# A hybrid encoder layer on one core: the three products of each split fp32 matmul in another order, and the zero matmuls of the v projection left out

## The chip, the cores and the metric

The kernel runs on one core of a Trainium2 chip. A core has a matrix engine (PE, with the loading of its weights shown apart as PEld), a vector engine (DVE), a scalar engine (ACT), a general engine (POOL) and a queue engine (SP) that issues the transfers between HBM and the on-chip memory. The metric is the device time of one execution in microseconds.

## What is computed

One encoder layer over two sequences, 1024 tokens (prompt) and 256 tokens (sample), width 2048, in fp32:

```python
def hybrid_layer(x, norm_w, w_in, na_rpb, conv_w, conv_b, gate_b, head_norm_w, w_out):
    hn = rmsnorm(x, norm_w)
    proj = jnp.einsum('btd,dp->btp', hn, w_in)
    na_q, na_k, na_v, na_g, ml_qk, ml_v, ml_o, ml_z, ml_gp = jnp.split(proj, cuts, axis=-1)
    att = neighbourhood_attention(na_q..., na_k..., na_v..., na_rpb)
    att = (att * jax.nn.silu(na_g)).astype(x.dtype)
    qk = jax.nn.silu(centred_depthwise_conv(ml_qk, conv_w, conv_b))
    ...
    h = bidirectional_mlstm(mq, mk, mv, gates)
    h = rmsnorm(h, head_norm_w...)
    mem = (h * jax.nn.sigmoid(ml_o) * jax.nn.silu(ml_z)).astype(x.dtype)
    mixed = jnp.concatenate([att, mem], axis=-1)
    return x + jnp.einsum('btm,md->btd', mixed, w_out)
```

The trunk ends with another RMSNorm. The two large products are `hn @ w_in` (2048 by 9232) and `mixed @ w_out` (2048 by 2048).

## The kernel before

Every fp32 product is made of three matmuls. An operand is split into a high half h, the value rounded to the matmul's reduced fp32 format (a cast on ACT), and a low half l, the rest (a subtraction on DVE); the product is h times h, plus h times l, plus l times h. The product of the two low halves is left out. In a matmul the stationary operand (128 by 128) is loaded into the engine, the moving operand (128 by up to 512 columns) is streamed through it, and the result is added up in one of eight banks of 512 fp32 columns per partition. Each matmul here comes with its own load of the stationary operand, also where that operand is the same as in the matmul before.

The tokens are taken in two groups: A, the first 768, and B, the last 512. The kernel has these stages, one after another on PE:

- Stage one projects group A (line 188, streams of 384 columns). The change doesn't touch it.
- The mixed stage, from about 1112 us, projects group B: the v columns by `proj_v` (names `wsv`, `pv`, line 583) and the others by `proj_pair` (names `ws`, `pc`, line 499). It does so beside attention and mLSTM of both sequences.
- The late gates are calls of `proj_pair` for gate columns that are applied at once.
- The output projection (`out_mm`, names `m_`, `ws_o`, `po`, line 1215) runs over three groups of 4, 4 and 2 token tiles of 128.

`proj_pair` makes two output tiles of 128 columns by 512 tokens, j = 0 and 1, each in a bank of its own, out of a ring of three banks (tag "pr"). The depth of 2048 is taken in four pieces r. For each piece SP loads 512 KB of weights into one of two buffers (`wr`), and `w_split` makes of each half of it, one for each j, a tile `ws` with high and low half: `t[:, 0]` starts the tile, `t[:, 1]` lies 544 columns on. The ring of these tiles has four places, shared with the tiles of `proj_v`. Here the weights are the stationary operand and the x tile, 512 tokens, the moving one. For each j the 12 matmuls of a piece run over four slices of depth with three products each, in the order (w0, xh), (w0, xl), (w1, xh), before the other j begins. When the pair ends, DVE takes both banks out with the scale of the tokens (line 165).

`out_mm` has the parts the other way round: the mixed activations `m` (128 tokens) are stationary and the output weights (512 columns) move, in the order (mh, w0), (mh, w1), (ml, w0). For each of four blocks of 512 columns and each slice of depth it runs over the token tiles of the group; the last four slices of depth (eight in the last block of the last group) are held back, and are run tile by tile, so that the tiles end one after another.

`proj_v` has x stationary and the weights moving with 256 columns. Two token tiles share a bank, so before the first product of a bank a matmul with a tile of zeros (`zer`, line 581) is written over all its 512 columns, with the start mark; the products then all add to it. For the head group that also makes the gates, each token tile has its own bank and there is no zero matmul.

The order in which the instructions stand on each engine isn't the written one: a scheduler places them by its own estimate of the times, within the dependencies. Within an engine they then run strictly in that order, and each waits for the counters that it was given.

Of the kernel before, what the change touches and what calls it, by code (L numbers as in the profile page):

```python
# [9 lines left out]
F32R = mybir.dt.float32r  # L10
# [3 lines left out]
P = 128  # L14
# [24 lines left out]
def kernel(  # L39
# [23 lines left out]
    def f(ap):  # L63
        return ap.bitcast(F32)
# [379 lines left out]
    for i, n1 in enumerate(order):  # L444
# [3 lines left out]
        k = i - 4  # L448
# [11 lines left out]
        tri(late.tile([P, P], F32, tag=n, name=n), cm, 0, (0.0, NEG))  # L460
        for n, cm in (("mask_f", -1), ("mask_b", 1))
    )
    zer = late.tile([P, P], F32R, tag="zer", name="zer")
    G.memset(f(zer), 0.0)

    xp1 = ctx.enter_context(tc.tile_pool(name="xp1", bufs=1))

# [11 lines left out]
    def w_split(raw, lo_, hi_, name, keep=False):  # L479
# [5 lines left out]
        split(t[:, 0, :n], t[:, 1, :n], raw[:, lo_:hi_])  # L485
        return t

    def proj_pair(n1, X, late=False):
        pb = [bank("pr", f"pc{n1}_{j}") for j in range(2)]
        for r in range(4):  # L490
            raw = w_piece(w_in[n1 // 2, r], f"{n1}_{r}")
            for j in range(2):
                t = w_split(raw, j * 512, j * 512 + 512, f"{n1}_{r}{j}")
                for f_ in range(2):
                    for q in range(2):
                        xh, xl = X.get(8 * f_ + 2 * r + q)
                        c = (2 * f_ + q) * P
                        for wi, xs in ((0, xh), (0, xl), (1, xh)):
                            PE.matmul(  # L499
                                pb[j], t[:, wi, c : c + P], xs,  # L500
                                start=r == 0 and f_ == 0 and q == 0 and wi == 0 and xs is xh,
                                stop=r == 3 and f_ == 1 and q == 1 and wi == 1,
                            )
        out = []
        for j in range(2):
            o = po(f"pco{n1}_{j}")
            if QK0 <= n1 < OT0:
                ct = n1 - QK0 + j
                DM.dma_start(o[:, 0:4], qb[ct])
                for z in (260, 518):  # L510
                    G.memset(o[:, z : z + 2], 0.0)
                out_scaled(
                    o[:, 4:].rearrange("p (s c) -> p s c", s=2)[:, :, :256],
                    pb[j].rearrange("p (s c) -> p s c", s=2),
                    rbs[1].rearrange("p (s c) -> p s c", s=2), n1,
                )
                cv = po(f"pcv{n1}_{j}")
                for _ in conv_taps(cv, o, ct, 516, 0):
                    pass
                DM.dma_start(cD[ct][:, GA - 2 : TP], cv[:, 0:258])  # L520
                DM.dma_start(cD[ct][:, TP:], cv[:, 260:516])
                continue
            o = o[:, :GB]
            out_scaled(o, pb[j], rbs[1], n1)
            if not late:
                DM.dma_start(pT[n1 + j][:, GA:], o)
            out.append(o)
        return out
# [21 lines left out]
    def proj_v(u, X):  # L550
        gates = u == NA_H // 2
        w = 272 if gates else 256
        nt = GB // P
        if gates:
            outs = [bank("a", f"pv{u}_{i}")[:, :w] for i in range(nt)]
        else:
            pb = [bank("pr", f"pv{u}_{i}") for i in range(nt // 2)]
            outs = [pb[t // 2][:, (t % 2) * 256 : (t % 2) * 256 + 256] for t in range(nt)]
        for r in range(4):
            raw = w_piece(w_in[NCH // 2 + u, r], f"v{u}_{r}")  # L560
            rawv = raw.rearrange("p (j f q c) -> p f q j c", j=2, f=2, q=2)
            if gates:
                graw = wb.tile([P, 2, 2, 16], F32, tag="wgr", name=f"wg{r}", bufs=2)
                DM.dma_start(
                    graw, w_g.rearrange("p (f r q c) -> p f r q c", f=2, r=4, q=2)[:, :, r]
                )
            for f_ in range(2):
                t = wb.tile([P, 2, 544], F32R, tag="wsp", name=f"wsv_{u}_{r}_{f_}", bufs=4)
                t4 = t[:, :, : 2 * w].rearrange("p h (k c) -> p h k c", k=2)
                h2, l2 = (  # L570
                    t4[:, z, :, 0:256].rearrange("p q (j c) -> p q j c", j=2) for z in range(2)
                )
                split(h2, l2, rawv[:, f_])
                if gates:
                    split(t4[:, 0, :, 256:272], t4[:, 1, :, 256:272], graw[:, f_])
                for tt in range(nt):
                    for q in range(2):
                        first, last = r + f_ + q == 0, r == 3 and f_ == 1 and q == 1
                        xh, xl = X.get(8 * f_ + 2 * r + q)
                        if first and not gates and tt % 2 == 0:  # L580
                            PE.matmul(pb[tt // 2], zer, t[:, 0, :512], start=True, stop=False)
                        for m, (xs, wi) in enumerate(((xh, 0), (xh, 1), (xl, 0))):
                            PE.matmul(  # L583
                                outs[tt],
                                xs[:, tt * P : (tt + 1) * P],
                                t[:, wi, q * w : (q + 1) * w],
                                start=first and m == 0 and gates,
                                stop=last and m == 2 and (gates or tt % 2 == 1),
                            )
        rc = rcs[1]  # L590
        for tt in range(nt):
            o = wb.tile([P, 256], F32, tag="vo", name=f"vo{u}_{tt}", bufs=2)
            S.mul(o, outs[tt][:, :256], rc[:, tt : tt + 1])
            r0 = GA + tt * P
            DM.dma_start(vD[u][r0 : r0 + P, :], o)
            if gates:
                V.scalar_tensor_tensor(
                    gt[:, GA // P + tt, :], outs[tt][:, 256:272], rc[:, tt : tt + 1], gb_sb,
                    op0=ALU.mult, op1=ALU.add,
                )  # L600
# [550 lines left out]
    X = LazyX()  # L1151
# [52 lines left out]
    for g, (t0, n) in enumerate(OG):  # L1204
        mh, ml_ = [None] * KT, [None] * KT
        for k in range(KT):
            raw = ahead[k] if g == 0 and k in ahead else mix_raw(g, k)
            mh[k], ml_[k] = x_pair(k, f"m{g}_{k}")
            split(mh[k][:, : n * P], ml_[k][:, : n * P], raw)
        yt = [yp.tile([P, D], F32, tag="y", name=f"y{g}_{t}", bufs=5) for t in range(n)]  # L1210
        ss = [yp.tile([P, 4], F32, tag="ss", name=f"ss{g}_{t}", bufs=8) for t in range(n)]

        def out_mm(o, tt, k, t, first, last):
            for i, (xs, wi) in enumerate(((mh[k], 0), (mh[k], 1), (ml_[k], 0))):
                PE.matmul(  # L1215
                    o, xs[:, tt * P : (tt + 1) * P], t[:, wi, :512],
                    start=first and i == 0, stop=last and i == 2,
                )

        for nb in range(4):  # L1220
            held = []
            n_hold = 8 if (g, nb) == (2, 3) else 4
            banks = [bank("pr" if nb % 2 and i < 3 else "a", f"po{g}_{nb}_{i}") for i in range(n)]
            for kp in range(0, KT, 2):
                nm = f"o{g}_{nb}_{kp}"
                raw = yp.tile([P, 1024], F32, tag="wr", name=f"wr_{nm}", bufs=4)
                DM.dma_start(raw, w_o[nb, :, kp * 512 : kp * 512 + 1024])
                for q in range(2):
                    k = kp + q
                    t = w_split(raw, q * 512, q * 512 + 512, f"{nm}_{q}", KT - n_hold <= kp < KT - 4)  # L1230
                    if kp >= KT - n_hold:
                        held.append((k, t))
                        continue
                    for tt in range(n):
                        out_mm(banks[tt], tt, k, t, k == 0, False)
            for tt in range(n):
                for i, (k, t) in enumerate(held):
                    out_mm(banks[tt], tt, k, t, False, i == n_hold - 1)
                cs = slice(nb * 512, nb * 512 + 512)
                xr = yp.tile([P, 512], F32, tag="xr", name=f"xr{g}_{nb}_{tt}", bufs=4)  # L1240
                DM.dma_start(xr, xtok[(t0 + tt) * P : (t0 + tt + 1) * P, cs])
                V.tensor_tensor(yt[tt][:, cs], banks[tt], xr, op=ALU.add)  # L1242
                S.activation(xr, yt[tt][:, cs], AF.Square, accum_out=ss[tt][:, nb : nb + 1])  # L1243
                G.tensor_tensor(yt[tt][:, cs], yt[tt][:, cs], fnb[:, cs], op=ALU.mult)  # L1244
                if nb == 3:
                    finish(t0 + tt, yt[tt], ss[tt])
# [87 lines left out]
```

## Time and profile before

| | |
|---|---|
| median of 3 runs | 2664.28 us (2663.93 to 2666.6) |
| profiled execution | 2667.78 us |
| its span, from the first instruction to the last | 2666.1 us |
| matmuls of `pc` | 2688 |
| matmuls of `po` | 1920 |
| matmuls of `pv` with 256 or 272 columns, and with zeros | 1536 and 14 |
| HBM read and written | 322.28 MB and 66.13 MB |

In the rows of the profile, L12 is line 12 of the kernel; names stand as output, arrow, inputs, with the buffer numbers left out, so that `pc<-x_4h,ws` are all matmuls with the high half of x slice 4 and some weight tile. `po<-ws_o,m_5l` has the low half of m slice 5. Duration of a matmul is modelled: they are pipelined, and one begins before the last one's duration ends, so that the spacing of the starts is what sets the pace. Rows of stretches give their length, then for PE, PEld, DVE, ACT and POOL busy time and number of instructions, then the granted clock, the share of the transfer engines and GB/s. Rows of the chain give start and length in us, the work and its count. Rows of one line or one tile give minimum, median and maximum duration in ns, and first and last start. Rows that begin with a cause give the idle time in us that the cause ended, and the number of cases.

### The profile page before, as it was taken

The numbers are of one execution on the slowest core, as the hardware profiler recorded it, in microseconds if no ns is written. First come the engines' busy times: TensorE is split into PE (matmuls) and PEld (weight loads), VectorE is DVE, ScalarE is ACT, GpSimd is POOL, SyncE is SP. The second block draws the span as 40 slices with busy tenths as digits, with TensorE's granted clock in tenths as the row PEclk, the third lists the DMA queues.
The fourth block names the chain that finished last, engine by engine and source line by source line (L and its number), as shares of the span: only waits on it lengthen the run. The fifth ranks groups of instructions, "written<-read, shape, count | busy, mean of one in ns | idle before, by whom it ended". The sixth has DMA issues, their size and how long they took to land. (4 is left out here: it accounts for less than half of the span.)

```text
span 2666.1 us, 42804 instructions
## 1 busy us (share of the span) xinstructions
PE 2627.4 (99%) x14724; PEld 2410.9 (90%) x14724; DVE 1804.6 (68%) x3645; ACT 1307.2 (49%) x2995; POOL 617.9 (23%) x898
## 2 busy tenths in 40 slices
PE   8999999999999999999999999999999999999998
PEld 8999999999999999988998998998888888888876
DVE  7867878788877878773686686686567445353455
ACT  7534444444444444543765665666556223242344
POOL 0434444444444444200010010110010000020121
PEclk9999999999999999999999999999999999999999
DMA  6423333323323233534555655655644545354465
GB/s 210 153 71 127 105 118 105 113 90 100 100 84 108 95 96 99 173 113 158 180 177 174 198 174 165 207 160 176 201 161 154 189 143 197 111 187 165 135 229 168
DMA packets 206435, 391.24 MB, mean 147 GB/s; under 512 B 25952, under 2 KB 117256, under 8 KB 206088
## 3 DMA queue, kind: packets, MB, share of 16 engines
q1 hardware_dynamic: 206216, 388.49, 45.4%
q8 instruction: 116, 1.90, 0.3%
q14 instruction: 103, 0.84, 0.1%
HBM read 322.28 MB, written 66.13 MB: 146 GB/s over the span
## 5 line engine op out<-in xcount | busy, mean ns | idle before, releaser
L152 DVE TENSOR_TENSOR ws_o<-wr_o,ws_o 128x512 fp32r<-128x512 f32 x192 | 150.5, 798 | 145.7 <-ACT ws_o L151 144.0
L152 DVE TENSOR_TENSOR ws<-wr,ws 128x512 fp32r<-128x512 f32 x224 | 154.7, 693 | 130.7 <-ACT ws L151 128.9
L151 ACT CAST ws<-wr 128x512 fp32r<-128x512 f32 x224 | 138.2, 619 | 187.7 <-PE pc L499 151.4
L151 ACT CAST ws_o<-wr_o 128x512 fp32r<-128x512 f32 x192 | 116.1, 617 | 165.9 <-PE po L1215 140.5
L1244 POOL TENSOR_TENSOR y<-y,fnb 128x512 f32<-128x512 f32 x40 | 58.5, 1479 | 536.2 <-ACT xr L1243 536.0
L1242 DVE TENSOR_TENSOR y<-po,xr 128x512 f32<-128x512 f32 x40 | 26.6, 685 | 50.7 <-PE po L1215 50.6
L152 DVE TENSOR_TENSOR wsv<-wr_v,wsv 128x512 fp32r<-128x512 f32 x64 | 45.3, 710 | 22.5 <-ACT wsv L151 22.0
L1243 ACT ACTIVATE xr<-y 128x512 f32<-128x512 f32 x40 | 25.1, 627 | 69.3 <-DVE y L1242 69.3
L102 POOL TENSOR_SCALAR mls_0r<-mls_0r 128x2 f32<-128x2 f32 x4 | 0.9, 234 | 249.4 <-ACT mls_0jk L1092 249.4
L151 ACT CAST wsv<-wr_v 128x512 fp32r<-128x512 f32 x64 | 39.2, 616 | 38.2 <-PE pc L499 25.1
L165 DVE TENSOR_TENSOR pco<-pc,rstdb 128x512 f32<-128x512 f32 x48 | 32.9, 686 | 29.2 <-PE pc L499 29.2
L274 DVE SCALAR_TENSOR_TENSOR pcv<-pco,cw_sb,pcv 128x516 f32<-128x516 f32 x64 | 47.8, 755 | 0.5 <-ACT pcv L268 0.5
L499 PE MATMUL pc<-x_8h,ws 128*128 128x512 f32 x112 | 44.5, 397 | 0.0
L499 PE MATMUL pc<-x_15h,ws 128*128 128x512 f32 x112 | 44.5, 397 | 0.0
L499 PE MATMUL pc<-x_10h,ws 128*128 128x512 f32 x112 | 44.5, 397 | 0.0
L499 PE MATMUL pc<-x_3h,ws 128*128 128x512 f32 x112 | 44.5, 397 | 0.0
L499 PE MATMUL pc<-x_0h,ws 128*128 128x512 f32 x112 | 44.4, 397 | 0.0
L499 PE MATMUL pc<-x_13h,ws 128*128 128x512 f32 x112 | 44.4, 396 | 0.0
L499 PE MATMUL pc<-x_4h,ws 128*128 128x512 f32 x112 | 44.4, 396 | 0.0
L499 PE MATMUL pc<-x_6h,ws 128*128 128x512 f32 x112 | 44.4, 396 | 0.0
L499 PE MATMUL pc<-x_9h,ws 128*128 128x512 f32 x112 | 44.4, 396 | 0.0
L499 PE MATMUL pc<-x_7h,ws 128*128 128x512 f32 x112 | 44.4, 396 | 0.0
(1737 smaller groups left out, 8901.4 us busy)
## 6 DMA issues: line engine op xcount, KB each, us to landing
wr<-in_w_in_dram SPq DMA_DIRECT2D x112, 512.0 KB
wr_o<-in_w_o_dram SPq DMA_DIRECT2D x96, 512.0 KB
wr_v<-in_w_in_dram SPq DMA_DIRECT2D x32, 512.0 KB
xq<-in_xtok_dram SPq DMA_DIRECT2D x20, 512.0 KB
xr<-in_xtok_dram SPq DMA_DIRECT2D x40, 256.0 KB
out_dram<-y SPq DMA_DIRECT2D x18, 512.0 KB
mraw<-mx SPq DMA_DIRECT2D x32, 256.0 KB
xr<-in_xT_dram SPq DMA_DIRECT2D x16, 384.0 KB
```

The costliest lines, as they stand in the source:

```text
L102: G.tensor_scalar(out, ssum, 1.0 / count, EPS, op0=ALU.mult, op1=ALU.add)
L151: S.copy(hi, src)
L152: V.tensor_tensor(lo, src, f(hi), op=ALU.subtract)
L165: V.tensor_tensor(o, src, rb, op=ALU.mult)
L274: V.scalar_tensor_tensor(dst[:, a:n], src[:, a + j - pad : n + j - pad], cw_sb[:, ct, j : j + 1], dst[:, a:n], op0=ALU.mult, op1=ALU.add,)
L499: PE.matmul(pb[j], t[:, wi, c : c + P], xs, start=r == 0 and f_ == 0 and q == 0 and wi == 0 and xs is xh, stop=r == 3 and f_ == 1 and q == ...
L1242: V.tensor_tensor(yt[tt][:, cs], banks[tt], xr, op=ALU.add)
L1243: S.activation(xr, yt[tt][:, cs], AF.Square, accum_out=ss[tt][:, nb : nb + 1])
L1244: G.tensor_tensor(yt[tt][:, cs], yt[tt][:, cs], fnb[:, cs], op=ALU.mult)
```

## The change

In `proj_pair` both tiles of a piece are split first. Then, for each slice of depth, three products of j = 0 and three of j = 1 follow each other, those of j = 1 in the opposite order: (w0, xl), (w0, xh), (w1, xh), then with the other tile (w1, xh), (w0, xh), (w0, xl). In `out_mm` the order is (ml, w0), (mh, w0), (mh, w1) for even token tiles and the reverse for odd ones. In `proj_v` the zero matmul goes; the first product of the even token tile in a bank carries the start mark, and the odd one adds to the same bank without one. The tile of zeros and its memset go.

```diff
-    zer = late.tile([P, P], F32R, tag="zer", name="zer")
-    G.memset(f(zer), 0.0)
...
+    FORTH = ((0, 1), (0, 0), (1, 0))
+
     def proj_pair(n1, X, late=False):
         pb = [bank("pr", f"pc{n1}_{j}") for j in range(2)]
         for r in range(4):
             raw = w_piece(w_in[n1 // 2, r], f"{n1}_{r}")
-            for j in range(2):
-                t = w_split(raw, j * 512, j * 512 + 512, f"{n1}_{r}{j}")
-                for f_ in range(2):
-                    for q in range(2):
-                        xh, xl = X.get(8 * f_ + 2 * r + q)
-                        c = (2 * f_ + q) * P
-                        for wi, xs in ((0, xh), (0, xl), (1, xh)):
+            t = [w_split(raw, j * 512, j * 512 + 512, f"{n1}_{r}{j}") for j in range(2)]
+            for f_ in range(2):
+                for q in range(2):
+                    xs = X.get(8 * f_ + 2 * r + q)
+                    c = (2 * f_ + q) * P
+                    first, last = r + f_ + q == 0, r == 3 and f_ == 1 and q == 1
+                    for j, passes in enumerate((FORTH, FORTH[::-1])):
+                        for m, (wi, xi) in enumerate(passes):
                             PE.matmul(
-                                pb[j], t[:, wi, c : c + P], xs,
-                                start=r == 0 and f_ == 0 and q == 0 and wi == 0 and xs is xh,
-                                stop=r == 3 and f_ == 1 and q == 1 and wi == 1,
+                                pb[j], t[j][:, wi, c : c + P], xs[xi],
+                                start=first and m == 0, stop=last and m == 2,
                             )
...
-                        if first and not gates and tt % 2 == 0:
-                            PE.matmul(pb[tt // 2], zer, t[:, 0, :512], start=True, stop=False)
                         for m, (xs, wi) in enumerate(((xh, 0), (xh, 1), (xl, 0))):
...
-                                start=first and m == 0 and gates,
+                                start=first and m == 0 and (gates or tt % 2 == 0),
...
         def out_mm(o, tt, k, t, first, last):
-            for i, (xs, wi) in enumerate(((mh[k], 0), (mh[k], 1), (ml_[k], 0))):
+            for i, (wi, xi) in enumerate(((1, 0), (0, 0), (0, 1))[:: 1 if tt % 2 else -1]):
                 PE.matmul(
-                    o, xs[:, tt * P : (tt + 1) * P], t[:, wi, :512],
+                    o, (mh[k], ml_[k])[xi][:, tt * P : (tt + 1) * P], t[:, wi, :512],
                     start=first and i == 0, stop=last and i == 2,
                 )
```

## The prediction

> **What bounds the kernel now.** I read the page first, then the kernel in five stretches, then the chain of work that ended last, and then single groups of matmuls.
>
> ```profile
> span 2666.1 us, 42804 instructions
> PE 2627.4 (99%) x14724; PEld 2410.9 (90%) x14724; DVE 1804.6 (68%) x3645; ACT 1307.2 (49%) x2995; POOL 617.9 (23%) x898
> PEclk9999999999999999999999999999999999999999
> ```
>
> PE is busy 99% of the span and its clock is granted in full. The next view cuts the span into stage one (projection of the first 768 tokens), the mixed stage (second projection beside attention and mLSTM), the late gates, two groups of the output projection, and the last group.
>
> ```profile
> 0.00:1112.30 1112.30, 1093.23 (x6271) 1083.56 (x6272) 870.59 (x1562) 528.01 (x1239) 467.66 (x560) 1.00 0.35 113
> 1112.30:2066.00 953.70, 947.28 (x5897) 849.88 (x5897) 656.84 (x1689) 567.59 (x1360) 81.67 (x278) 1.00 0.55 172
> 2066.00:2207.00 141.00, 141.00 (x625) 115.83 (x624) 60.31 (x93) 39.57 (x68) 0.00 (x0) 1.00 0.45 157
> 2207.00:2535.00 328.00, 327.93 (x1432) 268.03 (x1431) 144.83 (x196) 112.20 (x217) 44.74 (x36) 1.00 0.51 163
> 2535.00:2666.00 131.00, 117.98 (x504) 93.58 (x503) 72.03 (x107) 59.84 (x113) 23.82 (x24) 0.97 0.59 198
> ```
>
> After the length stands PE's busy time. PE idles 6.4 us of the 953.7 in the mixed stage, nothing in the late gates, 0.1 in the first output groups, 13 in the last. So from 1112 us on the time is the number of matmuls times their spacing, and waits are worth little. The chain says the same, and from it the mean spacing can be had (start, length, instruction, count):
>
> ```profile
> 1994.62 5.46 DMA wr<-in_w_in_dram
> 2079.18 131.12 PE pc L499 x567
> 2210.30 173.77 PE po L1215 x759
> 2387.15 174.62 PE po L1215 x761
> ```
>
> The gate projection (pc) runs 567 matmuls at 131.12/567 = 231.3 ns, the output projection (po) 759 at 229.0 ns. Both stream 512 columns, in threes, so the difference must come from the order of the operands. The durations in undisturbed stretches show where (min/median/max):
>
> ```profile
> L499 PE MATMUL pc<-x_11h,ws x17: 389/397/397, 2110.1 to 2198.8; 128*128 128x512 f32 x17
> L499 PE MATMUL pc<-x_4h,ws x16: 389/393/397, 2110.3 to 2180.1; 128*128 128x512 f32 x16
> L499 PE MATMUL pc<-x_11l,ws x9: 396/396/396, 2109.8 to 2198.6; 128*128 128x512 f32 x9
> L1215 PE MATMUL po<-ws_o,m_5h x64: 389/392/395, 2223.9 to 2534.4; 128*128 128x512 f32 x64
> L1215 PE MATMUL po<-ws_o,m_5l x32: 388/388/388, 2224.3 to 2534.6; 128*128 128x512 f32 x32
> L188 PE MATMUL A58b<-xg,A58s x144: 334/334/335, 307.8 to 335.7; 128*128 128x384 f32 x144
> ```
>
> A modelled duration is the spacing to the next start plus a constant: in pc the three are 389, 396 and 397, mean 394, less 231.3 gives 162.7; in po 389, 395, 388, mean 390.7, less 229.0 gives 161.7. So there are two classes of step, some 227 ns and some 234, and I call the second dear. Write w0 and w1 for the high and low half of a weight tile (w0 starts the tile, w1 lies 544 columns on) and h, l for the halves of x. In pc the order is (w0,h) 389, (w0,l) 396, (w1,h) 397: the step into w1 and the step out of w1 are dear. In po it is (h,w0) 389, (h,w1) 395, (l,w0) 388: only the step out of w1 is dear. The last row but one says more: all 32 l matmuls took 388, those too that end a weight tile, after which both operands change. So a change of both operands alone isn't what costs. Stage one, with the same three products at 384 columns and its halves otherwise placed, has one class, 334.
>
> **The change part by part.** First, the zero matmuls:
>
> ```profile
> L581 PE MATMUL pv<-wsv,zer x14: 389/394/397, 1190.9 to 1773.9; 128*128 128x512 f32 x14
> ```
>
> 14 of them at 394 - 162 = 232 ns: 3.2 us off PE, in the mixed stage, where nothing else is the bound. The tile's memset on POOL goes too; POOL is busy 23% of the span and waits there, so I count nothing (uncovered, it would be a part of a microsecond, once). The v projection keeps its order otherwise.
>
> Second, the pair projection. The 2688 matmuls, 224 casts, 224 subtracts and 112 loads of weights stay. What moves is the order, which a scheduler makes; in the built program I counted steps between neighbouring pc matmuls. Steps between w0 and w1 fall from 836 in and 833 out to 515 and 524, since two w1 now stand side by side. That is 630 dear steps fewer at 396.5 - 389 = 7.5 ns: 4.7 us. Steps where both operands change fall from 1671 to 554. Bounds of this term: nothing (if each use of a w1 or l tile costs its 7.5 ns wherever it stands), and 1117 x 7.5 = 8.4 us (if every change of both costs). I take the middle, which is what the rows of both projections obey together; it is a rule read off, and its mechanism I don't know.
>
> Third, the output projection: 1920 matmuls, steps out of w1 fall from 630 to 354: 276 at 395 - 388.5 = 6.5 ns, 1.8 us. Bounds: nothing; and 630 - 44 = 586 steps that leave w1 with both operands changed, 3.8 us.
>
> What the new orders ask of others. A block of 24 matmuls now needs both tiles of a piece and frees both at its end, where before each was freed after its 12. Rows for the preparation:
>
> ```profile
> L151 ACT CAST ws<-wr x224: 602/621/660, 1132.9 to 2199.2; 128x512 fp32r<-128x512 f32 x112
> L152 DVE TENSOR_TENSOR ws<-wr,ws x224: 652/691/965, 1133.6 to 2199.9; 128x512 fp32r<-128x512 f32 x112
>   PE pc L499: 152.5, 96
>   DMA wr<-in_w_in_dram: 27.9, 12
> ```
>
> The last two rows tell what the idle engine waited for ahead of these: 152.5 us in 96 cases for PE to give a tile back, 27.9 us in 12 for the load. So preparation is mostly early. A block lasts 24 x 0.231 = 5.5 us; two casts and the last subtract take 2 x 0.62 + 0.69 = 1.9 us. With four tiles in the ring, the pair freed at the end of one block is refilled during the next, with 3.6 us to spare: nothing on the path. Without that cover the loss would be up to 1.9 us for each of 112 pieces.
>
> A pair also starts its second bank sooner after the last pair ended, and that bank waits for DVE to empty it:
>
> ```profile
> L165 DVE TENSOR_TENSOR pco<-pc,rstdb x48: 670/690/693, 1161.7 to 2210.3; 128x512 f32<-128x512 f32 x48
> ```
>
> In the written order this would be six matmuls, 1.4 us, against 0.69 us plus whatever DVE has in hand. In the built order of the late gates 14 matmuls of the first bank go ahead, 3.2 us, so again nothing; if one in four of the 28 pairs lost 0.7 us, 5 us.
>
> In the output projection the first matmul of an even tile now needs the low half of x, which DVE makes, and the low half of the weights only third instead of second. The waits that PE had:
>
> ```profile
> PE po L1215 <- DVE ws_o L152: 3.1, 5, 1.0
> PE mlp_1in L924 <- ACT mlp_1Cb L151: 1.7, 2, 1.1
> ```
>
> Five waits for that low half become up to two spacings shorter (at most 1.2 us gained), three group starts up to 0.7 us longer (2.1 lost): counted as nothing.
>
> Sum: 3.2 + 4.7 + 1.8 = 9.7 us. The profiled execution took 2667.8 us, 3.5 above the median of the runs shown, 2664.3; against its own time the forecast is 2658, against the median 2654.5.
>
> **A rule weighed.** The durations above split into two classes 7 ns apart by the order of operands. The Trainium skill (TensorE: Matmul & The Clock Gate, "Part 2: What happens when you issue a matmul") says that the next weights are loaded ahead into a background buffer, through a read port of their own, so that a new stationary operand takes nothing from the running stream. By that rule no order is dearer and only the zero matmuls count; its gap for 512 columns, N/2.4 + 2.5 = 216 ns, is also below every spacing here (227 to 234), so the trace so far does not bear it out in full. It is the first rival.
>
> **The rivals.** (1) Order doesn't matter: each stream costs by what it streams, dear ones stay dear wherever they stand. For it: in po every use of w1 as the moving operand is dear, and nearly no w1 follows a w1 there. Against: l as the moving operand is dear in pc, l as the stationary one in po isn't. Then 3.2 us: 2661. (2) Every change of both operands is dear. For it: pc has two of three such steps and both are dear. Against: the l rows of po. Then 3.2 + 8.4 + 3.8 = 15.4: 2649. (3) Slower: the load of a piece comes late and PE stands. The 12 waits of 27.9 us above are ACT's; PE lost only 1.7 us to the chain behind one (ACT mlp_1Cb), because other matmuls stood between. In the chain a load of weights took 5.46 us. Load, two casts and a subtract are 7.4 us against two blocks, 11.1 us, so it decides from the point at which SP issues a load over 3.7 us late, as SP does where it queues behind loads for attention. If all of the 27.9 reach PE, less 9.7: +18 us, 2682; half of them, 2668. (4) The change doesn't do what it says: the scheduler breaks up the written order. It does in part (554 changes of both instead of the 448 as written), and the counts above have this in them.
>
> **How the numbers follow.** My forecast of 2654.5 has 0.38, with a range of its own from 2650 to 2658 (its two terms off by half); rival 1 has 0.26, rival 2 0.22, rival 3 0.14. The range from 2647 to 2667 takes in rivals 1 and 2 with some 2 us of waits either way and the milder end of rival 3; outside stay most of rival 3 and gains beyond rival 2, about 0.17. About 0.2%, 5.3 us, is what a measurement of this kernel can tell from no change, so faster means below 2659: forecast and rival 2, with a little off for waits that eat into it and a little from rival 1, 0.62. Rival 1 and the mild end of rival 3 give 0.26 for the same, the rest 0.12 for slower.
>
> **What would show it.** The long stretch of gate matmuls should go from 231.3 to about 229.5 ns each (231.3 under rival 1, 228 under rival 2), the output stretches from 229.0 to about 228. In the gate rows the low half of x should have 388 or 389 where another product with w0 follows. The group with zer is gone. Idle time of PE from 1112 to 2066 us should stay near 6 us; 15 or more there, ended by ws, speaks for rival 3. I am wrong on the size if both spacings stay, and on the sign if PE's waits for ws grow by over 10 us.

## The result and the profile after

The changed kernel takes 2682.34 us (median of six runs, 2675.46 to 2684.13) against 2664.11 us for the kernel before (six runs, 2662.57 to 2668.24). The ratio is 1.0062, with a 95% interval from 1.0049 to 1.0075: slower by 0.6%. It is worked out from the single runs; the two medians alone give 18.2 us, or 1.0068. The forecast was 2654.5, with a range up to 2667.

The page of the changed kernel begins so:

```profile
span 2680.8 us, 42790 instructions
PE 2631.7 (98%) x14710; PEld 2407.5 (90%) x14710; DVE 1797.0 (67%) x3645; ACT 1307.0 (49%) x2995; POOL 617.9 (23%) x897
PEclk9999999999999999999999999999999999999999
```

The 14 zero matmuls are gone (14710 instead of 14724), the clock is granted in full as before, and the span is 14.7 us longer (2680.8 less 2666.1). That is less than the 18.2 us between the medians, since the profiled execution of the kernel before took 2667.78 us, 3.7 above its median; the traces below explain the 14.7. Each matmul still has its own load of weights, 14710 of 14710, also where it keeps the weights of the one before.

The view by stretches, cut as before (length; busy us and count of PE, PEld, DVE, ACT, POOL):

```profile
0.00:1112.30 1112.30, 1091.33 (x6268) 1080.63 (x6269) 866.98 (x1563) 528.36 (x1240) 469.06 (x560) 1.00 0.35 113
1112.30:2066.00 953.70, 940.78 (x5829) 841.07 (x5828) 649.89 (x1672) 558.00 (x1340) 79.83 (x277) 1.00 0.55 171
2066.00:2207.00 141.00, 141.00 (x643) 115.66 (x642) 62.79 (x105) 44.69 (x83) 0.00 (x0) 1.00 0.49 164
2207.00:2535.00 328.00, 327.20 (x1415) 265.30 (x1414) 138.43 (x190) 111.15 (x211) 43.06 (x36) 1.00 0.48 155
```

In the mixed stage PE idles 953.7 - 940.8 = 12.9 us; it was 6.4. In the output stretch it is busy nearly all the time, and yet fewer matmuls get through: 1415 instead of 1432. So there are two losses of different kinds, one of waits and one of pace. The chain of waits (start, length, instruction, count) tells them apart:

```profile
2091.68 128.48 PE pc L500 x553
2220.16 173.16 PE po L1213 x749
...
2402.22 173.50 PE po L1213 x749
```

The long run of output matmuls starts at 2220.16 instead of 2210.30: 9.9 us are lost ahead of it, and 14.7 - 9.9 = 4.8 us behind it. The gate matmuls now stand 128.48/553 = 232.3 ns apart, where 231.3 was before and 229.5 the forecast; the output matmuls 173.16/749 = 231.2, where 229.0 was before and 228 the forecast. Both got slower, not faster. Rows of single groups (minimum, median and maximum duration):

```profile
L500 PE MATMUL pc<-x_11h,ws x24: 392/397/404, 2096.2 to 2208.4; 128*128 128x512 f32 x24
L500 PE MATMUL pc<-x_11l,ws x12: 387/389/397, 2096.0 to 2208.6; 128*128 128x512 f32 x12
L500 PE MATMUL pc<-x_4l,ws x12: 389/395/397, 2097.4 to 2210.9; 128*128 128x512 f32 x12
L1213 PE MATMUL po<-ws_o,m_5h x56: 387/393/397, 2233.8 to 2503.6; 128*128 128x512 f32 x56
L1213 PE MATMUL po<-ws_o,m_5l x28: 388/394/398, 2234.3 to 2503.8; 128*128 128x512 f32 x28
```

Before, the durations fell into two narrow classes. Now single groups spread over 10 ns and more (387 to 397, 392 to 404), and the low halves of m, which all took 388, have a median of 394. One group did as forecast: the low half of x_11 went from 396 to 389. On the whole the cheap steps became dearer, and the dear ones didn't go away.

The starts of neighbouring matmuls in the traces show which steps these are. The table gives the mean distance from one start to the next, in ns, for slices of depth whose matmuls stand in a row in their full written order, each under 260 ns from the next; w1' and w0' belong to the other tile, m' to the next token tile.

```text
pair projection    before (701 slices): (w0,h) to (w0,l) 228.1; to (w1,h) 232.4; to the next slice 233.6
                   after (183 slices):  (w0,l) to (w0,h) 230.1; to (w1,h) 231.6; to (w1',h) 235.3;
                                        to (w0',h) 233.2; to (w0',l) 233.6; to the next slice 231.0
output projection  before (451 slices): (h,w0) to (h,w1) 227.4; to (l,w0) 233.7; to the next 226.1
                   after (215 pairs):   (l,w0) to (h,w0) 229.1; to (h,w1) 231.0; to (h',w1) 232.4;
                                        to (h',w0) 230.2; to (l',w0) 227.5; to the next 234.8
```

Two w1 side by side, which the prediction counted as steps saved, are the dearest step of the new pair projection: 235.3 ns on average, with a median of 237, where the dear steps before took 232.4 and 233.6.

For sums over a whole stage, "spacing" in the next table is what a matmul's distance to the next start is above columns/2.4 + 13.3 ns (226.6 ns for 512 columns), added up over all those where that is under 60 ns; "pauses" adds up the others, of matmuls with 128 columns or more. A pause need not be idle time, since the modelled duration of a matmul reaches beyond the start of the next: of 31.6 us after, PE counts as idle in 12.9. All is in us; "mixed" runs from the first matmul of v to the first of the output, "output" from there to the last matmul.

```text
kernel          mixed   pc spacing  pauses   output  po spacing
before          1097.7     13.0      21.1     445.6     4.9
after           1107.0     15.0      31.6     450.5     8.5
e1_out          1097.7     13.0      21.2     450.2     8.4
e2_proj         1102.7     14.8      24.8     446.4     5.1
e3_zero         1095.2     13.0      22.4     446.0     4.9
e8_proj_zero    1108.2     15.0      33.1     446.5     5.4
e7_blocks12     1099.5     13.7      25.9     450.0     8.5
e4_align        1089.2      4.8      18.7     442.1     0.6
e9_low2048      1089.5      4.9      21.2     442.1     0.6
e10_low2112     1094.5     12.6      18.7     450.8    10.2
e5_after_align  1101.6      4.9      34.3     444.0     0.5
e6_zero_align   1089.9      4.9      22.8     441.8     0.5
e11_vo1         1103.8     15.8      28.2     452.2     9.5
e12_raw3        1097.8     15.7      22.0     452.2     9.6
```

So from before to after, the mixed stage has -3.2 for the zero matmuls, +2.0 in spacing and +10.5 in pauses: +9.3. The output stage has +3.6 in spacing and 1.3 in other places: +4.9. The other 0.5 us of the span lies ahead of the mixed stage, in work that the change doesn't touch; there single traces differ by more (1111.8 us in e9, 1115.4 in e2), so the table rather than the span is to be compared. Each row is one trace.

### The profile page after: what moved, and what is told of

It reads as the page before. It is cut to its first block, busy times and chain, and to the rows that moved or that the text cites. A ratio compares the mean times of both kernels' runs of the same rounds, so it can differ in the third digit from the quotient of the medians.

```text
span 2680.8 us, 42790 instructions
## 1 busy us (share of the span) xinstructions
PE 2631.7 (98%) x14710; PEld 2407.5 (90%) x14710; DVE 1797.0 (67%) x3645; ACT 1307.0 (49%) x2995; POOL 617.9 (23%) x897
## 4 chain that ended last, share of the span: by engine, by line
PE 51%; DMA 4%; DVE 3%; ACT 1%; issue 1%; SPq 0%; POOL 0%; ACTq 0%; POOLq 0%; DVEq 0%
PE pc L500 20%; PE po L1213 16%; PE pv L581 5%; PE A54b L188 1%; PE A52b L188 1%; DMA wr<-in_w_in_dram 1%; PE nap_0s L618 1%; PE nap_1s L618 1%; DMA nap_0vr<-vD 0%; DMA mlp_0zr<-pT 0%; DMA wr_o<-in_w_o_dram 0%; PE nap_1o L744 0%; PE nap_0t L635 0%; PE nap_1t L635 0%; PE nap_0o L744 0%
## 5 line engine op out<-in xcount | busy, mean ns | idle before, releaser
L151 ACT CAST wsv<-wr_v 128x512 fp32r<-128x512 f32 x64 | 38.8, 616 | 31.6 <-PE pc L500 19.3
L500 PE MATMUL pc<-x_0h,ws 128*128 128x512 f32 x112 | 36.0, 401 | 0.9 <-DVE pco L165 0.9
L188 PE MATMUL fb<-xg,fw 128*128 128x384 f32 x192 | 35.1, 336 | 1.7 <-ACT xg L158 1.7
L500 PE MATMUL pc<-x_2h,ws 128*128 128x512 f32 x112 | 35.4, 399 | 0.0
L188 PEld LDWEIGHTS fb<-xg,fw 128*128 128x128 f32 x192 | 33.3, 188 | 2.2 <-ACT xg L158 2.2
L500 PE MATMUL pc<-x_8h,ws 128*128 128x512 f32 x112 | 34.6, 396 | 0.0
L500 PE MATMUL pc<-x_1h,ws 128*128 128x512 f32 x112 | 34.4, 395 | 0.0
L188 PE MATMUL fb<-xb,fw 128*128 128x384 f32 x96 | 23.2, 355 | 11.0 <-ACT xb L158 11.0
L500 PE MATMUL pc<-x_9h,ws 128*128 128x512 f32 x112 | 33.7, 397 | 0.0
L500 PE MATMUL pc<-x_5h,ws 128*128 128x512 f32 x112 | 33.1, 397 | 0.0
L500 PE MATMUL pc<-x_4h,ws 128*128 128x512 f32 x112 | 33.1, 397 | 0.0
```

The lines of the kernel that those rows point to most:

```text
L151: S.copy(hi, src)
L188: PE.matmul(o, w(a_), x(b_), start=first and m == 0, stop=last and m == 2)
L500: PE.matmul(pb[j], t[j][:, wi, c : c + P], xs[xi], start=first and m == 0, stop=last and m == 2,)
```

## The experiments

The kernels e1 to e8 ran on one chip in two batches (the kernel before took 2668.08 us beside e1 to e4 and 2667.78 beside e5 to e8), e9 to e12 on another (2667.39). Each ratio is to the kernel before of its own batch.

### One part at a time

**e1_out**: the kernel before, with the new order in the output projection only.

```diff
-            for i, (xs, wi) in enumerate(((mh[k], 0), (mh[k], 1), (ml_[k], 0))):
+            for i, (wi, xi) in enumerate(((1, 0), (0, 0), (0, 1))[:: 1 if tt % 2 else -1]):
...
```

> Only the output projection has the new order of operands. Theory of the prediction (steps out of the low weight half are dear): 1.8 us faster, ratio 0.9993. Rival A (the new order itself runs slower on PE, as the trace of the whole change suggests: 231.2 to 231.6 ns in its long output stretches against 229.0 to 229.5): 4 to 5 us slower, 1.0017. Rival B (the loss is all in the mixed stage): no change, 1.0000.

Measured: 2673.09 us, ratio 1.0017 (1.0008 to 1.0026). The output order alone costs 4.5 us by the ratio, and the table has all of it in the output stage (+4.6), with the spacing of the whole change.

**e2_proj**: the kernel before, with the new pair projection only.

```diff
-            for j in range(2):
-                t = w_split(raw, j * 512, j * 512 + 512, f"{n1}_{r}{j}")
...
+            t = [w_split(raw, j * 512, j * 512 + 512, f"{n1}_{r}{j}") for j in range(2)]
...
+                    for j, passes in enumerate((FORTH, FORTH[::-1])):
...
```

> Only the pair projection has the new order and both tiles of a piece ahead. Theory of the prediction: 4.7 us faster, 0.9982. Rival A (spacing of the gate matmuls goes from 231.3 to about 232.5 ns, nothing else): 3 us slower, 1.0012. Rival B (waits in the mixed stage, where the scheduler places attention and mLSTM otherwise around the longer blocks): 8 to 14 us slower, 1.003 to 1.005.

Measured: 2674.09 us, ratio 1.0021 (1.0012 to 1.003), between the two rivals of the expectation. The chain view of e1 and then of e2:

```profile
2080.39 131.12 PE pc L499 x567
2211.51 173.14 PE po L1215 x749
```

```profile
2089.70 128.48 PE pc L502 x553
2218.18 173.94 PE po L1217 x759
```

Each part moves only its own pace: in e1 gates 231.3 and output 231.2, in e2 gates 232.3 and output 229.2.

**e3_zero**: the kernel before, with the zero matmuls left out and nothing else.

```diff
-    zer = late.tile([P, P], F32R, tag="zer", name="zer")
-    G.memset(f(zer), 0.0)
...
-                        if first and not gates and tt % 2 == 0:
-                            PE.matmul(pb[tt // 2], zer, t[:, 0, :512], start=True, stop=False)
...
-                                start=first and m == 0 and gates,
+                                start=first and m == 0 and (gates or tt % 2 == 0),
```

> Only the 14 zero matmuls are left out. Theory of the prediction: 14 x 232 ns = 3.2 us faster, 0.9988. Rival (the mixed stage is placed anew and loses by waits what PE gains): no change or up to 5 us slower, 1.0000 to 1.0020.

Measured: 2666.79 us, ratio 0.9994 (0.9985 to 1.0003). The interval holds both nothing and the 3.2 us forecast; in the trace the mixed stage is 2.5 us shorter.

The three parts give 5.0 + 6.0 - 1.3 = 9.7 us by their medians; the whole change gave 18.2 (by the ratios, 0.32% and 0.62%). That the parts disturb each other shows in **e8_proj_zero**, the changed kernel with the old order of the output projection:

```diff
-            for i, (wi, xi) in enumerate(((1, 0), (0, 0), (0, 1))[:: 1 if tt % 2 else -1]):
+            for i, (xs, wi) in enumerate(((mh[k], 0), (mh[k], 1), (ml_[k], 0))):
...
```

> The changed kernel with the old order in the output projection: new pair projection and no zero matmuls. If the parts add, 5.6 - 1.6 = 4 us over the kernel before, 1.0015. If the two disturb each other through the scheduler's placing of the mixed stage, as the whole change's profile has it (9.3 us longer before the output projection, the two alone 5.0 and -2.5): 9 to 12 us, 1.0035 to 1.0045.

Measured: 2680.86 us, ratio 1.0044 (1.0031 to 1.0056). The mixed stage takes 1108.2 us, though e2 and e3 alone would make it 1097.7 + 5.0 - 2.5 = 1100.2. The surplus of 8 us is in the pauses (33.1 against 24.8 in e2). Between e2 and e8 only the zero matmuls went; what else differs is the order that the scheduler made around them. Why that order is the worse one wasn't settled.

### What makes a step dear

Both products read the low half of a weight tile 2176 B (544 columns) behind the high half, that is 8.5 times 256 B. In stage one, whose 384-column steps were all alike, the halves of a weight tile are 1024 B apart. **e4_align** is the kernel before with the low half 2304 B on, nine times 256 B; the instructions keep their order on every engine.

```diff
-            t = wb.tile([P, 2, 544], F32R, tag="wsp", name=f"ws_{name}", bufs=4)
+            t = wb.tile([P, 2, 576], F32R, tag="wsp", name=f"ws_{name}", bufs=4)
```

(The same size stands in the tile of `proj_v`.)

> The kernel before, but with the low half of each weight tile 576 instead of 544 columns behind the high half (2304 bytes, a multiple of 256, instead of 2176). If the place of the low half makes the dear steps, they go: 1669 steps of the pair projection at 7.5 ns and 630 of the output projection at 6.5 ns, 16.6 us faster, 0.9938, with 227 ns spacing everywhere. If the order of operands makes them: no change, 1.0000, with the same 227 and 234 ns.

Measured: 2659.43 us, ratio 0.9961 (0.9949 to 0.9974). The dear steps went, but the gain is short of the 16.6 us expected. In the table the spacing falls by 8.2 us in the pair projection, where 12.5 were expected, and by 4.3 in the output projection. And the v projection, whose low half e4 moves too, became slower: the mean distance between its 256-column matmuls is 119.6 ns in e4 and 117.8 before (1242 neighbours in each trace), 2.3 us in all.

**e5_after_align** is the same edit in the changed kernel, again with every engine's order unchanged:

> The changed kernel with the low half of each weight tile 2304 instead of 2176 bytes behind the high half. Theory A (the odd place makes the steps dear in either order, and the new order only meets it more often): all 512-column steps are 227 ns, the stretch of gate matmuls goes from 232.3 to 227, the output stretches from 231.4 to 227, some 18 us off, about 2664, ratio to the kernel before 1.000. Theory B (the new order is dear in itself): spacing stays above 230 ns, ratio 1.004 or more. What is left above the kernel before with the same placing (2659) is the price of waits in the mixed stage.

Measured: 2669.95 us, ratio 1.0006 (0.9998 to 1.0015). The chain view of e4 and then of e5:

```profile
2075.02 128.62 PE pc L499 x567
2203.63 172.05 PE po L1215 x759
```

```profile
2088.78 125.43 PE pc L500 x553
2214.20 169.79 PE po L1213 x749
```

Gates 226.8 and output 226.7 ns, in the old order and in the new: with this placement no dear step is left in these two products, and the order of operands sets nothing in their pace. A row of e5 shows it for the group that spread from 387 to 397 above:

```profile
L1213 PE MATMUL po<-ws_o,m_5h x56: 388/390/390, 2227.6 to 2492.3; 128*128 128x512 f32 x56
```

Yet e5 stays 10.5 us above e4. In the mixed stage, which is 12.4 us longer in e5 (1101.6 and 1089.2), there are 15.6 us more of pauses, less 3.2 for the zero matmuls. So the better placement does away with the loss of pace and not with the waits.

The larger tile might also have moved other tiles, so **e9_low2048** and **e10_low2112** keep tile, ring and every address but that of the low half in `proj_pair` and `out_mm`: 2048 B on in e9 (512 columns), 2112 B in e10 (528; there the cut is at 1056). Both are the kernel before otherwise, with the order of instructions on every engine unchanged, and leave the v projection at 2176 B.

```diff
...
             t = wb.tile([P, 2, 544], F32R, tag="wsp", name=f"ws_{name}", bufs=4)
+            t = t.rearrange("p z c -> p (z c)")[:, : 1024].rearrange("p (z c) -> p z c", z=2)
```

> The kernel before, with the low half of each weight tile of the gate and output projections put 2048 B (512 columns) behind the high half instead of 2176 B; the tile keeps its size and its base, and so do all other tiles; the v projection keeps 2176 B. Theory A (a step is dear when the two halves stand an odd multiple of 128 B apart from a multiple of 256): 2048 is a multiple of 256, so gate steps of 226 to 227.5 ns and output steps of 226 to 227.5, as with 2304 B, and about 2660 against 2668 for the kernel before. Rival B (the larger tile of e4 moved the bases of the tiles, or of those behind it, and that did it): spacings stay at 231 and 229, and the time within 2 us of before.

> The same with the low half 2112 B (528 columns) behind the high half, 64 B off a multiple of 256. Theory A as a rule of 256 B: dear steps again, gate and output spacings over 228 ns (231 and 229 if 64 off costs what 128 off costs, in between if the cost grows with the offset), time 2662 to 2668. If what counts is a multiple of 64 B: 226 to 227.5, about 2660, and then 2176 B, also a multiple of 64, would have to be dear for another reason.

Measured: e9 2656.25 us, ratio 0.9963 (0.9949 to 0.9976); e10 2672.33 us, ratio 1.002 (1.0011 to 1.0028). The chain view of e9 and then of e10:

```profile
2072.83 128.62 PE pc L500 x567
2201.45 172.05 PE po L1216 x759
```

```profile
2076.83 131.10 PE pc L500 x567
2207.93 176.03 PE po L1216 x759
```

With 2048 B, 226.8 and 226.7 ns; with 2112 B, 231.2 and 231.9. So it is the place of the low half: in the 512-column products two distances that are multiples of 256 B are cheap in every step, two that aren't (2112 and 2176) are not. The output pace at 2112 B is worse than at 2176, and e10 is slower than the kernel before, where 2662 to 2668 us were expected; so it isn't one price for "off". Nor is a multiple of 256 B better everywhere: e9, with its v projection at 2176 B, keeps the 117.8 ns there that e4 lost. The tiles themselves are 4352 B long (4608 in e4), multiples of 256 as well, so these runs can't tell the distance between the halves from the address of the low half. Why it matters stays open, as does whether another placement of the x halves would.

### What makes the pauses

**e7_blocks12**: the changed kernel, but each tile's 12 matmuls of a piece as a block again (the order of the three products within it stays as changed).

```diff
-            t = [w_split(raw, j * 512, j * 512 + 512, f"{n1}_{r}{j}") for j in range(2)]
...
+            for j, passes in enumerate((FORTH, FORTH[::-1])):
+                t = w_split(raw, j * 512, j * 512 + 512, f"{n1}_{r}{j}")
```

> The changed kernel, but in the pair projection each tile's 12 matmuls run as a block of their own again, with the orders (w0,xl), (w0,xh), (w1,xh) for the first tile and the reverse for the second. Theory A (blocks of 24 that need and free two tiles at once make the waits of the mixed stage): the mixed stage loses its extra 6 to 9 us, what is left is the output projection's 4.5 less the zero matmuls: ratio 1.001 to 1.002. Rival (any new order makes the scheduler place the mixed stage anew, and worse): 1.004 to 1.006.

Measured: 2675.36 us, ratio 1.0026 (1.0017 to 1.0035), against 1.0062 for the whole change: 0.0036 of 2668, about 9.6 us, or 5 to 14 with both intervals. In the trace 7.5 us of it are in the mixed stage, 5.7 of these in pauses and 1.3 in spacing. So over half of the added pauses went with the block of 24, which takes and returns two tiles at a time. That the hand-over of two tiles makes them is argued and not shown: the scheduler made another order of all the work for e7 too, and no run has more tiles in the ring.

How a pause comes about shows in a stretch of the changed kernel's timeline (start, length, engine, line, work; in brackets the idle time before it and what ended it), SP's queue first, then ACT and PE:

```profile
1385.01 2.33 SPq L727 DMA_DIRECT2D nap_2vr<-vD  x4
1387.39 1.13 SPq L474 DMA_DIRECT2D wr<-in_w_in_dram  x2
```

```profile
1387.26 0.48 ACT L1055 ACTIVATE mlp_1x<-mlp_1in,mgpei 128x258 f32<-128x258 f32 x1
1393.34 0.62 ACT L151 CAST ws<-wr 128x512 fp32r<-128x512 f32 x1 [5.60 <-DMA wr<-in_w_in_dram]
1393.86 0.84 ACT L1055 ACTIVATE mlp_1x<-mlp_1in,mgpei 128x258 f32<-128x258 f32 x2
```

```profile
1394.38 0.81 PE L618 MATMUL nap_0s<-nap1qk 128*128 128x384 f32 x3 [1.73 <-ACT mlp_1x L1055]
```

SP issues the loads for attention ahead of the weights. ACT stands at the cast of a weight tile for 5.6 us until that load lands, and what is behind the cast in its queue, two evictions `mlp_1x` of mLSTM, stands too. PE runs out of other work and idles 1.73 us for one of these evictions. So the idle time bears the name of the mLSTM, not of the weights. Over the whole mixed stage, the groups of that cast, before and then after (count, busy us, mean ns, idle us ahead of it and what ended it):

```profile
L151 ACT CAST ws<-wr 128x512 fp32r<-128x512 f32 x177 | 109.1, 619 | 100.0 <-PE pc L499 75.1 <-DMA wr<-in_w_in_dram 23.6 <-ACT nap5o L757 0.7
```

```profile
L151 ACT CAST ws<-wr 128x512 fp32r<-128x512 f32 x174 | 106.0, 617 | 93.8 <-PE pc L500 60.5 <-DMA wr<-in_w_in_dram 27.3 <-PE pv L581 4.5
```

and the waits behind these sums (us in all, times, longest), before and after:

```profile
ACT ws L151 <- PE pc L499: 75.1, 57, 3.8
```

```profile
ACT ws L151 <- PE pc L500: 60.5, 30, 6.0
ACT ws L151 <- DMA wr<-in_w_in_dram: 27.3, 8, 5.7
```

ACT doesn't wait longer in all; it waits less often and longer each time: 2.0 us instead of 1.3 for a tile that PE gives back. To test the load by itself, it has to come earlier. To make room for a third buffer for raw weights two others are given up, so there are two kernels: **e11_vo1**, the changed kernel with fewer buffers elsewhere, as a control, and **e12_raw3**, the control with the third buffer.

```diff
-NRA, NWS, NWT, NPC, NPO = 3, 8, 4, 5, 6
+NRA, NWS, NWT, NPC, NPO = 3, 8, 4, 5, 5
...
-            o = wb.tile([P, 256], F32, tag="vo", name=f"vo{u}_{tt}", bufs=2)
+            o = wb.tile([P, 256], F32, tag="vo", name=f"vo{u}_{tt}", bufs=1)
```

```diff
-        raw = wb.tile([P, 1024], F32, tag="wraw", name=f"wr_{name}", bufs=2)
+        raw = wb.tile([P, 1024], F32, tag="wraw", name=f"wr_{name}", bufs=3)
```

> A control for the next run: the kernel after with five buffers instead of six for streamed x and output tiles, and one instead of two for the evicted v tile, which makes room in on-chip memory. Either theory: slower than after by 0 to 10 us (2680 to 2692), since evictions of v wait for the store of the one before.

> The control with three instead of two buffers for the raw weight pieces, so that a load is issued a piece earlier. Theory A (PE stands in the mixed stage because a cast of weights waits in ScalarE's queue for its load, and other work queues behind it): 4 us or more faster than the control, casts waiting on the load for under 10 us in all instead of 27, PE's idle time from 1112 to 2066 us 4 us or more lower. Rival B (the waits come from tiles that PE gives back a pair at a time, and the load is early enough in what PE sees): within 2 us of the control, PE's idle time as there.

Measured: e11 2681.59 us, ratio 1.0054 (1.0041 to 1.0067); e12 2675.64 us, ratio 1.0034 (1.0022 to 1.0047). The five runs of e12 (2674.61 to 2678.9) lie all below the five of the control (2679.15 to 2684.61). The mixed stretch and the group of the cast, e11 and then e12:

```profile
1112.30:2066.00 953.70, 943.84 (x5851) 842.38 (x5850) 649.99 (x1681) 562.23 (x1351) 77.13 (x277) 1.00 0.55 172
L151 ACT CAST ws<-wr 128x512 fp32r<-128x512 f32 x175 | 106.4, 618 | 81.7 <-PE pc L500 43.9 <-DMA wr<-in_w_in_dram 30.2 <-PE pv L581 4.0
```

```profile
1112.30:2066.00 953.70, 948.55 (x5888) 846.71 (x5887) 657.97 (x1689) 567.32 (x1360) 82.05 (x277) 1.00 0.55 173
L151 ACT CAST ws<-wr 128x512 fp32r<-128x512 f32 x176 | 107.1, 618 | 53.5 <-PE pc L500 40.7 <-PE pv L581 9.5 <-DMA pT<-pco 2.2
```

The 30.2 us that casts waited for loads are gone from the row, the wait for PE's tiles stays (43.9 and 40.7), and PE's idle time falls from 9.9 to 5.2 us; the kernel is 6.0 us faster. So late loads made about 6 us of the pauses. The scheduler made a new order for e12 too, so a part of the 6 us may be its own. Nor are these 6 us shown to be part of what the change added: the kernel before had nearly as much of this wait (23.6 us, 27.3 after), and a third buffer there wasn't run.

### A version that beats both

**e6_zero_align**: the kernel before, with its old order of operands, without the zero matmuls and with the low half 2304 B on (the edits of e3 and e4).

> The kernel before with the low half 2304 bytes behind and the 14 zero matmuls left out, in the old order. Theory A: the gains of the two single runs add, 10.5 and 1.6 us, ratio 0.9955. If the new placement of the mixed stage by the scheduler eats the zero matmuls' gain: 0.9961.

Measured: 2656.9 us (2654.66 to 2658.65), ratio 0.9957 (0.9944 to 0.9969). It is 0.4% faster than before. The part that counts is the placement: e9, which has only that, has the ratio 0.9963. Whether leaving out the zero matmuls adds anything stays open, since the interval holds both values of the expectation.

## Why the prediction was wrong

- **The zero matmuls, 3.2 us.** They went, and alone they bring between -0.8 and 4.0 us (e3's interval). Together with the new pair projection that gain is not seen: e8 isn't faster than e2.
- **The pair projection, -4.7 us, and the output projection, -1.8 us.** Here the prediction failed first: it took 630 steps between w0 and w1 as saved "since two w1 now stand side by side", and so priced the step from one w1 to the other as cheap. The kernel before has hardly any such step, so no row of it gave a price. It took 235.3 ns on average in the pair projection, more than the steps that it replaced (232.4 and 233.6), and the cheap steps rose too: where (w0,h) to (w0,l) took 228.1, no step of the new order is under 230.1. In the output projection the step between two w1 took 232.4 ns and the steps beside it 231.0 and 230.2, so that four steps in six are over 230 ns, where one in three was. The rule behind the price, that a step into or out of the low half w1 costs 7.5 or 6.5 ns, was drawn from two orders, each with one repeating pattern; "its mechanism I don't know", as the prediction says. What decides whether order matters is where w1 lies (e4, e9, e10). Measured is +2.0 and +3.6 us in spacing. The bounds failed with it: both began at nothing, and no row excluded a loss. (The forecast's own range, with both terms off by half, would also begin at 2651 and not at 2650.) The row of stage one, one class at 384 columns with "halves otherwise placed", was quoted in the prediction and pointed to the placement; I used it only to note the difference.
- **Both tiles of a piece in one block, "nothing on the path".** The second failed step, worth more than the first: +10.5 us of pauses in the mixed stage. The sum, 1.9 us of splitting in a block of 5.5, holds only where the load is there and ACT is free for the casts. In the chain of waits the load was on the path before the late gates already (5.46 us), and the cast holds up whatever stands behind it on ACT. Breaking up the block again gives back some 9.6 us (e7), an earlier load about 6 (e12 against e11); how much of the 10.5 each of them explains isn't separated from the scheduler's new orders.
- **The second bank's eviction, nothing.** Right: `pc` waits once for `pco`, 0.9 us in all.

```profile
PE pc L500 <- DVE pco L165: 0.9, 1, 0.9
PE po L1213 <- DVE ws_o L152: 3.2, 4, 1.5
PE po L1213 <- ACT ws_o L151: 2.1, 1, 2.1
```

- **Start of the output groups, counted as nothing.** Roughly right: 3.2 us in four waits for the low half of the output weights, against 3.1 in five, and one wait of 2.1 for a high half, which is new. The 1.2 us that the prediction allows for five waits is one spacing for each, and not two as it says.
- **The rivals.** Rival 1 (each stream costs by what it streams) fails at the l rows of the output, 388 before and 394 after. Rival 2 (only a change of both operands is dear) fails as well: such changes became fewer and the spacing grew. Rival 3 named the sign, the time of 2682 and the point from which it decides, loads that SP issues late behind those for attention; I gave it 0.14 because before PE had lost only 1.7 us to it. But its sum, all 27.9 us less 9.7, met the time by chance: the real one is 10.5 us of pauses and 5.6 of spacing less 3.2, and some 2 of other items. The scheduler (rival 4) matters in another way than I had it: not by breaking up the triples, but by making a different order of all the work for each edit; with it the mixed stage of e8 is 8 us longer than the sum of e2 and e3.
- **The rule of the Trainium skill** (TensorE: Matmul & The Clock Gate, "Part 2: What happens when you issue a matmul"), that a new stationary operand costs the stream nothing since it is loaded ahead through a port of its own: with the low half 2304 B on the trace agrees, 226.8 ns in both orders (e4, e5), though that is still above the 216 ns that the prediction takes from there. At 2176 and 2112 B the spacing does depend on order and place, 229.0 to 232.7 ns in the long stretches, and there the measurement decides.

What would have shown it did: the spacings and the idle time of PE in the mixed stage (12.9 us, short of the 15 that I set as the mark of rival 3). But I said that these waits would be ended by `ws`, and that 10 us more of them would show the sign to be wrong. The sign was wrong, and `ws` by name ends 0.5 us, in the list of PE's waits in that stage:

```profile
PE mlp_1in L922 <- ACT mlp_1Cf L151: 2.9, 2, 2.2
PE nap_0s L618 <- ACT mlp_1x L1055: 1.7, 1, 1.7
PE pc L500 <- ACT ws L151: 0.5, 1, 0.5
```

The second is the one of the timeline above, where `mlp_1x` stands behind `ws` on ACT.

## What to carry to other kernels

When steps of the same shape differ by a few per cent, vary the place of the operands before their order: one line that moved the low half was worth 9 to 11 us here by the medians, while the change cost 18. Do it for each product by itself, since the placement that helped the 512-column products here cost the 256-column one 2.3 us. A block that needs two buffers at once had about half as many waits for a hand-over here, each of them longer (57 of 1.3 us became 30 of 2.0), so ask not whether the preparation fits on average, but what is queued behind it on its in-order engine when its load is late. Price a reordering from below nothing too, and test its parts together: their sum was half of the whole.

## What the runs showed that I had not expected

- In the long stretches of gate matmuls and in the first one of output matmuls, a 512-column matmul took 226.7 to 226.8 ns in both orders with the halves 2304 B apart, and in the old order with 2048 B; with 2112 or 2176 B it took 229.0 to 232.7 ns. The 256-column matmuls of v went the other way: 117.8 ns at 2176 B, 119.6 at 2304.
- Keeping an operand from one matmul to the next saved nothing that can be seen, neither the stationary one (it was loaded again each time, 14710 loads for 14710 matmuls) nor the moving one (226.7 ns with and without, the halves 2304 B apart).
- Leaving out 14 matmuls (3.2 us of work) and changing an order together made a mixed stage 8 us longer than the two alone would, with another order of everything else; that this order is the cause is inferred.
